# A two-layer encoder trunk on one core: two gate/up groups of three FFN stages taken together by Strassen's scheme, and weights split 1024 columns at a time

## The chip, the core and the metric

The kernel is one program on one core of a Trainium2 chip. The metric is the device time of one execution in microseconds (us), lower is better. Three runs of the kernel before are shown below, beside one profiled execution.

## What is computed

The input x has 256 tokens of 1024 values. Each of the two layers does: a half-step SwiGLU block, a mixer (self attention and attention to a memory, with one input and one output projection), and a second half-step SwiGLU block.

```
def swiglu(h, w_gate, w_up, w_down):
    return (jax.nn.silu(h @ w_gate) * (h @ w_up)) @ w_down
...
    h = rmsnorm(x, ffn1_norm[i])
    x = x + 0.5 * swiglu(h, ffn1_w_gate[i], ffn1_w_up[i], ffn1_w_down[i])
...
    h = rmsnorm(x, ffn2_norm[i])
    x = x + 0.5 * swiglu(h, ffn2_w_gate[i], ffn2_w_up[i], ffn2_w_down[i])
```

The gate and up weights are 1024 x 2816 each, the down weights 2816 x 1024, all in float32. There are four SwiGLU stages, called here (0,1), (0,2), (1,1) and (1,2) by layer and block.

## The kernel before, in words

**Precision.** Every float32 operand of a product is split into a high part (a cast to fp32r, on ScalarE) and a low part (the difference, on VectorE). `dense` (L405 to L425) then issues three matmuls for one tile of 128 x 128 by 128 x 512: high x high (L416), high x low (L419), low x high (L422).

**Weights.** A chunk is 128 x 2048 float32 (1 MB): four K tiles of 512 columns. `loader` brings chunks into three raw buffers (`NRAW`) with two DMAs of 512 KB each on SP's queue (L281). `split_hi` casts them in four pieces of 512 columns on ScalarE (L321), `split_lo` subtracts in the same four pieces on VectorE (L340). The results go to a ring of four high and four low buffers (`NHL`). So a split can run at most four chunks ahead of TensorE, and a raw buffer comes free when its last low part is written.

**A gate/up stage** has 11 groups of 256 gate and 256 up columns (put side by side, 512 wide), two chunks each (K tiles 0 to 3 and 4 to 7). For each chunk TensorE does two token blocks x four K tiles x three matmuls, 24 in all, into two PSUM banks per group. `evac` then does SiLU (ScalarE, L526), the product (VectorE, L529) and a block transpose (VectorE, L537), writes the result to DRAM (`hd`, L543) and reads it back turned (`hr`, L548), both on SP's queue between the loads of weights. The result is split again (L557, L559).

**The down stage** reads 11 more chunks. Three of them in each of the last three stages (`SEVEN`) are already taken by Strassen's scheme: seven products in place of eight, with weight sums on VectorE (L334).

**What sets the order.** The kernel's author wrote a planner into the program: `Flow` keeps a clock with assumed durations, threads (`loader`, `split_hi`, `split_lo`, `evac`, the mixer's units) are resumed by it, and the order in which they issue is the fixed order of every engine's and queue's instructions. On the chip each of these is taken strictly in that order, and an instruction whose operand isn't there holds up all behind it on its engine. `calm_a` and `calm_v` let a split in only when the planner sees at most 0.4 us of work queued on its engine.

**The side of x.** `prep_half` (L453 to L470) transposes x by TensorE, multiplies by the gain into `y` (L460), casts to `xh` (L463) and subtracts to `xl` (L465).

## Time and profile before

| | |
|---|---|
| Three runs | 964.70, 964.88 (median), 967.41 us |
| Profiled execution | 964.95 us, of which the span of the profile is 963.2 us |
| TensorE busy | 954.8 us (99%), clock granted 1.00 |
| VectorE busy | 745.0 us (77%) |
| ScalarE busy | 567.9 us (59%) |
| DMA | 204.04 MB, 212 GB/s over the span |

In time order the stages lie at about: (0,1) 12 to 195 us, first mixer 195 to 317, (0,2) 317 to 498, (1,1) 498 to 680, second mixer 680 to 781, (1,2) 781 to 963. PE is TensorE, DVE VectorE, ACT ScalarE, POOL GpSimd; SP's queue issues all loads. Matmuls overlap in the pipe, so the mean duration of one is longer than the distance from one to the next; the cost of a matmul in a stream is that distance.

### The profile page before, as it was taken

Reading aid. Unit: us, or ns where it says so; the run is one execution under the profiler, and the core shown is the slowest. Engines: PE = TensorE matmul, PEld = TensorE weight load, DVE = VectorE, ACT = ScalarE, POOL = GpSimd, SP = SyncE. Lnnn points to the kernel's source line nnn. Section 1 sums busy time; section 2 is a strip of 40 time slices with the busy share of each in tenths; the row PEclk is TensorE's granted clock in tenths of the full one; section 3 lists DMA queues with packets and bytes.
Section 4 is the critical chain, followed back from the end, with each engine's and each line's share of the span. In section 5 each row is a group of like instructions: output and inputs, shape, how many; then the busy total and the mean of one; then the engine's idle time right before and its main releaser. Section 6 shows DMA issues by size and latency. Waiting matters only on the chain.

```text
span 963.2 us, 13464 instructions
## 1 busy us (share of the span) xinstructions
PE 954.8 (99%) x4525; PEld 783.9 (81%) x4525; DVE 745.0 (77%) x1569; ACT 567.9 (59%) x1215; POOL 60.5 (6%) x65
## 2 busy tenths in 40 slices
PE   8999999999999999999999999999999999999998
PEld 7888888888777888888888888888787788888886
DVE  6777777788777877759986775797989886776785
ACT  6655555666676655545645555565677765554551
POOL 0000000021210000000000000000343100000000
PEclk9999999999999999999999999999999999999999
DMA  8988877486525479766568777666641468777661
GB/s 282 328 267 285 250 263 246 145 272 208 176 88 175 154 224 284 235 229 205 184 208 254 247 245 220 212 202 219 207 143 44 134 196 283 232 254 225 215 190 44
DMA packets 169295, 204.04 MB, mean 212 GB/s; under 512 B 9673, under 2 KB 144394, under 8 KB 169226
## 3 DMA queue, kind: packets, MB, share of 16 engines
q1 hardware_dynamic: 169226, 203.18, 66.0%
q8 instruction: 35, 0.57, 0.2%
q14 instruction: 34, 0.28, 0.1%
HBM read 188.99 MB, written 14.16 MB: 211 GB/s over the span
## 4 chain that ended last, share of the span: by engine, by line
PE 94%; DVE 3%; ACT 1%; DMA 1%; SPq 0%; issue 0%; ACTq 0%
PE gu L422 17%; PE gu L416 17%; PE gu L419 17%; PE acc L416 9%; PE acc L422 9%; PE acc L419 9%; PE pj L422 3%; PE pj L416 3%; PE pj L419 3%; PE xtp L429 1%; PE ptp L429 1%; PE S L1139 1%; PE AV L1220 1%; PE m L422 1%; PE m L419 1%; PE m L416 1%
## 5 line engine op out<-in xcount | busy, mean ns | idle before, releaser
L340 DVE TENSOR_TENSOR lo<-raw,hi 128x512 fp32r<-128x512 f32 x647 | 413.7, 684 | 103.9 <-ACT hi L321 100.0
L321 ACT CAST hi<-raw 128x512 fp32r<-128x512 f32 x647 | 361.7, 618 | 219.0 <-PE gu L422 123.6
L422 PE MATMUL gu<-hi,xl 128*128 128x512 f32 x704 | 274.3, 390 | 0.0
L416 PE MATMUL gu<-hi,xh 128*128 128x512 f32 x704 | 274.1, 389 | 0.0
L419 PE MATMUL gu<-lo,xh 128*128 128x512 f32 x704 | 274.0, 389 | 0.0
L422 PEld LDWEIGHTS gu<-hi,xl 128*128 128x128 f32 x704 | 132.2, 188 | 27.4
L419 PEld LDWEIGHTS gu<-lo,xh 128*128 128x128 f32 x704 | 132.2, 188 | 27.3
L416 PEld LDWEIGHTS gu<-hi,xh 128*128 128x128 f32 x704 | 132.2, 188 | 27.3
L416 PE MATMUL acc<-hi,ht 128*128 128x512 f32 x280 | 109.6, 391 | 0.0
L422 PE MATMUL acc<-hi,ht 128*128 128x512 f32 x280 | 109.2, 390 | 0.0
L419 PE MATMUL acc<-lo,ht 128*128 128x512 f32 x280 | 109.1, 390 | 0.0
L422 PE MATMUL pj<-hi,xl 128*128 128x512 f32 x160 | 64.5, 403 | 0.0
L419 PE MATMUL pj<-lo,xh 128*128 128x512 f32 x160 | 63.6, 397 | 0.0
L416 PE MATMUL pj<-hi,xh 128*128 128x512 f32 x160 | 63.5, 397 | 0.0
L422 PEld LDWEIGHTS acc<-hi,ht 128*128 128x128 f32 x280 | 52.6, 188 | 11.0
L419 PEld LDWEIGHTS acc<-lo,ht 128*128 128x128 f32 x280 | 52.6, 188 | 10.7
L416 PEld LDWEIGHTS acc<-hi,ht 128*128 128x128 f32 x280 | 52.6, 188 | 10.7
L526 ACT ACTIVATE sil<-gu,xr 128x256 f32<-128x256 f32 x88 | 41.5, 472 | 28.6 <-PE gu L422 28.6
L559 DVE TENSOR_TENSOR ht<-hr,ht 128x512 fp32r<-128x512 f32 x35 | 24.1, 687 | 32.2 <-ACT ht L557 32.2
L529 DVE SCALAR_TENSOR_TENSOR h<-gu,xr,sil 128x256 f32<-128x256 f32 x88 | 42.2, 479 | 5.8 <-ACT sil L526 4.5
L557 ACT CAST ht<-hr 128x512 fp32r<-128x512 f32 x35 | 21.6, 618 | 41.9 <-DMA hr<-hd 41.8
L436 POOL TENSOR_TENSOR xr<-v,nhalf 128x1 f32<-128x1 f32 x12 | 8.4, 698 | 502.3 <-DVE v L434 502.3
(191 smaller groups left out, 1069.0 us busy)
## 6 DMA issues: line engine op xcount, KB each, us to landing
raw<-in_ffn_w_down_dram SPq DMA_DIRECT2D x176, 256.0 KB, 4.1
raw<-in_ffn_w_gate_dram SPq DMA_DIRECT2D x86, 512.0 KB, 4.3
raw<-in_ffn_w_up_dram SPq DMA_DIRECT2D x86, 512.0 KB, 5.5
raw<-in_w_in_dram SPq DMA_DIRECT2D x32, 512.0 KB, 4.1
hd<-hb SPq DMA_DIRECT2D x44, 256.0 KB, 2.3
hr<-hd SPq DMA_DIRECT2D x44, 256.0 KB, 5.3
raw<-in_w_out_dram SPq DMA_DIRECT2D x8, 1024.0 KB, 5.0
raw<-in_w_mem_kv_dram SPq DMA_DIRECT2D x4, 1024.0 KB, 5.4
```

The costliest lines, as they stand in the source:

```text
L321: nc.scalar.copy(out=c.part(0, q), in_=c.block(q))
L340: nc.vector.tensor_sub(c.part(1, q), c.block(q), c.part(0, q).bitcast(F32))
L416: nc.tensor.matmul(out=ps, lhsT=xh, rhs=wh, start=start, stop=False)
L419: nc.tensor.matmul(out=ps, lhsT=xh, rhs=wl, start=False, stop=False)
L422: nc.tensor.matmul(out=ps, lhsT=xl, rhs=wh, start=False, stop=stop)
L429: nc.tensor.transpose(out=dst, in_=src, identity=flip if flipped else ident)
L526: nc.scalar.activation(sil, ps[tb][:, 0:256], AF.Silu, scale=xt.r[tb])
L529: nc.vector.scalar_tensor_tensor(out=h, in0=ps[tb][:, 256:512], scalar=xt.r[tb], in1=sil, op0=ALU.mult, op1=ALU.mult)
L557: nc.scalar.copy(out=hi, in_=src)
L559: nc.vector.tensor_sub(lo, src, hi.bitcast(F32))
L1139: nc.tensor.matmul(out=ss[e][:, pr, :nk], lhsT=q[rows, pr, :], rhs=k[rows, pr, :], start=i == 0, stop=i == len(passes) - 1)
L1220: nc.tensor.matmul(out=av[64 * e:64 * e + 64, pr, :], lhsT=vsrc(kb, pr, e), rhs=pts[e][:, pr, kb, :], start=(kb == 0), stop=(kb == nb - 1))
```

## The change

Two things are changed.

**Strassen in the gate/up stage.** In stages (0,2), (1,1) and (1,2), groups 3 and 4 are computed together (`PAIR`). Their weights are four chunks: 11 (group 3, K tiles 0 to 3), 21 (group 3, K tiles 4 to 7), 12 (group 4, K tiles 0 to 3) and 22 (group 4, K tiles 4 to 7). With the two token blocks on the other side this is a 2 x 2 by 2 x 2 product, done in seven products of four K tiles x three matmuls (12 each) in place of eight. Three of the right sides are plain chunks, four are sums T1 = 12 - 11, T3 = 22 - 12, T2 = 22 - T1 and T4 = 21 - T2 (`wsum`), made on VectorE in float32 four pieces at a time and split like a chunk. Each of these seven fills one of the four buffers of the high/low ring. Four forms of x are made at the start of the stage (`pair_forms`: four sums of `y`, four casts, four differences). The seven products `m1` to `m7` each go to a PSUM bank of their own, and `pair_sums` adds them up (one copy on ScalarE, seven additions on VectorE) before the usual evacuation. Groups 0 to 2 go ahead of the pair as before; chunks of groups 5 to 8 stand between its products (called p in the order: 11, m1, p, 12, m5, p, 22, m7, p, m6, p, m3, p, p, 21, m2, p, m4). Raw chunks 11, 12 and 22 stay in their raw buffers until a later product has read them too.

**Width of a split.** All chunks but the first two, and but the sums, are cast and subtracted 1024 columns at a time in place of 512.

```diff
@@ the weight blocks and the two splitting threads
+    class Item:
+        def __init__(self, raws, uses=8):
+            self.raws, self.uses = raws, uses
+            self.hi = self.lo = None
+            self.hit, self.lot, self.st = [None] * 7, [None] * 7, [None] * 4
+            self.n, self.frees, self.takes, self.gives = 1, 1, 0, 0
+            self.sums, self.t = [], []
+            self.index = len(items)
+            w = 1 if len(items) < 2 else 2
+            self.units = [(self.own(q, w), q, w, None) for q in range(0, 4, w)]
+            items.append(self)
+        def own(self, q, w=1, i=0):
+            return lambda: self.raws[i].raw[:, q * 512:(q + w) * 512]
+        def part(self, lo, q, w=1):
+            t = (self.lo if lo else self.hi)[q // 4]
+            return t[:, q % 4 * 512:(q % 4 + w) * 512]
+    chunks, items = [], []
...
-            for q in range(7 if c.seven else 4):
+        for i, it in enumerate(items):
+            yield lambda: hl_left[0] >= it.n and all(r.raw is not None for r in it.raws)
+            hl_left[0] -= it.n
+            yield max(r.early or r.arrive for r in it.raws)
+            it.hi, it.lo = ([whl.tile([P, 2048], F32R, tag=x, name=f"{x}{i}_{j}") for j in range(it.n)]
+                            for x in ("hi", "lo"))
+            for src, q, w, dep in it.units:
                 if q == 2:
-                    yield c.arrive
-                if c.seven and q >= 3:
-                    yield lambda: c.tt[q - 3] is not None
-                    yield c.tt[q - 3]
+                    yield max(r.arrive for r in it.raws)
+                if dep is not None:
+                    yield lambda: it.st[dep] is not None
+                    yield it.st[dep]
                 yield calm_a(i)
-                nc.scalar.copy(out=c.part(0, q), in_=c.block(q))
-                c.hit[q] = flow.act(512)
+                nc.scalar.copy(out=it.part(0, q, w), in_=src())
+                t = flow.act(512 * w)
+                it.hit[q:q + w] = [t] * w
...
+            if it.sums:
+                yield lambda: all(r.raw is not None for r in it.raws) and g2.left >= it.takes + 2
+                yield max(r.arrive for r in it.raws)
+                it.t += [g2.take([P, 512], F32, "wsum") for _ in range(it.takes)]
+                for j, (x, y) in enumerate(it.sums):
                     yield calm_v(i)
-                    nc.vector.tensor_sub(t[j], x, y)
-                    c.tt[j] = flow.dve(512)
-            for q in range(7 if c.seven else 4):
-                yield lambda: c.hit[q] is not None
-                yield c.hit[q]
+                    nc.vector.tensor_sub(it.t[j], x(), y())
+                    it.st[j] = flow.dve(512)
+            for src, q, w, dep in it.units:
+                yield lambda: it.hit[q] is not None
+                yield it.hit[q]
                 yield calm_v(i)
-                nc.vector.tensor_sub(c.part(1, q), c.block(q), c.part(0, q).bitcast(F32))
-                c.lot[q] = flow.dve(512)
-                if q == 3:
-                    raw_left[0] += 1
-            if c.seven:
-                g2.give(4)
+                nc.vector.tensor_sub(it.part(1, q, w), src(), it.part(0, q, w).bitcast(F32))
+                t = flow.dve(512 * w)
+                it.lot[q:q + w] = [t] * w
+            raw_left[0] += it.frees
+            g2.give(it.gives)
@@ which groups, and the products
+    PAIR = {(0, 1): None, (0, 2): 3, (1, 1): 3, (1, 2): 3}
...
+    def pair_items(raws):
+        r11, r12, r22, r21 = raws
+        def sums(need, x, y, held=None):
+            it = Item(need, 4)
+            it.t, it.takes = (held.t, 0) if held else ([], 4)
+            at_ = lambda v, j: it.own(j, 1, v) if isinstance(v, int) else (lambda: v.t[j])
+            it.sums = [(at_(x, j), at_(y, j)) for j in range(4)]
+            it.units = [((lambda j=j: it.t[j]), j, 1, j) for j in range(4)]
+            return it
...
+        def m1():
+            made["b11"] = plain(r11, 0)
+        def m5():
+            made["t1"] = sums([r12, r11], 0, 1)
+        def m7():
+            made["t3"] = sums([r22, r12], 0, 1)
+            made["t3"].gives = 4
+        def m6():
+            made["t2"] = sums([r22], 0, made["t1"], made["t1"])
+            made["t2"].frees = 0
+        def m3():
+            made["b22"] = plain(r22, 1)
+        def m2():
+            made["b21"] = plain(r21, 0)
+        def m4():
+            made["t4"] = sums([r21], 0, made["t2"], made["t2"])
+            made["t4"].gives = 4
+        return made, dict(m1=m1, m5=m5, m7=m7, m6=m6, m3=m3, m2=m2, m4=m4)
@@ the order of the blocks in a gate/up stage
+            rest = [w for w in work if w[0] not in (pair, pair + 1)]
+            n = 2 * pair
+            p = iter(rest[n:])
+            work = rest[:n]
+            for x in ("11", "m1", "p", "12", "m5", "p", "22", "m7", "p", "m6", "p", "m3", "p", "p", "21", "m2", "p", "m4"):
+                work.append(next(p) if x == "p" else x)
+            work += list(p)
+            blocks = {"11": (pair, 0), "12": (pair + 1, 0), "22": (pair + 1, 1), "21": (pair, 1)}
+            raws = [Chunk(parts(*blocks[x])) for x in ("11", "12", "22", "21")]
@@ the sides of x, the sums of the products and one product
+            yield lambda: len(xt.y) == 4 and g4.left >= 4
+            y = xt.y
+            fm = [g4.take([P, 2, 4, P], F32R, "xf") for _ in range(4)]
+            for j, op, o, a, b in ((0, nc.vector.tensor_add, (1, 1), (1, 0), (1, 1)),
+                                   (2, nc.vector.tensor_sub, (1, 0), (0, 0), (1, 0)),
+                                   (1, nc.vector.tensor_sub, (0, 0), (1, 1), (0, 0)),
+                                   (3, nc.vector.tensor_sub, (0, 1), (0, 1), (0, 0))):
+                yield lambda: flow.free["V"] <= flow.now + SLACK
+                op(y[o], y[a], y[b])
+                flow.dve(512)
+            for j, o in ((0, (1, 1)), (2, (1, 0)), (1, (0, 0)), (3, (0, 1))):
+                yield lambda: flow.free["A"] <= flow.now + SLACK
+                nc.scalar.copy(out=fm[j][:, 0], in_=y[o])
+                yield flow.act(512)
+                yield lambda: flow.free["V"] <= flow.now + SLACK
+                nc.vector.tensor_sub(fm[j][:, 1], y[o], fm[j].bitcast(F32)[:, 0])
+                xt.ft[j] = flow.dve(512)
+                g2.give()
+            xt.fm = fm
...
+            yield lambda: "m6" in mt and "m7" in mt
+            yield mt["m6"]
+            yield g2.has(3)
+            u2, w, v = (g2.take([P, 512], F32, "gu_v") for _ in range(3))
+            plus(u2, u, pb["m6"])
+            banks.give()
+            plus(w, u2, pb["m5"])
+            banks.give()
+            t = plus(v, w, pb["m7"])
+            pps[1][1], pend[1][1] = v, t
+            plus(u2, u2, pb["m7"])
+            banks.give()
+            for m, (g, tb), x in (("m3", (1, 0), w), ("m2", (0, 0), u), ("m4", (0, 1), u2)):
+                yield lambda: m in mt
+                yield mt[m]
+                t = plus(x, x, pb[m])
+                banks.give()
+                pps[g][tb], pend[g][tb] = x, t
...
+            name, left = {"m1": ("b11", (0, 0)), "m5": ("t1", 0), "m7": ("t3", 2), "m6": ("t2", 1), "m3": ("b22", 3),
+                          "m2": ("b21", (0, 1)), "m4": ("t4", (1, 1))}[m]
...
+                if isinstance(left, int):
+                    flow.until(lambda: xt.ft[left] is not None)
+                    f = xt.fm[left]
+                    fh, fl, ready = f[:, 0, k, :], f[:, 1, k, :], lambda: xt.ft[left]
+                else:
+                    tb, kk = left[0], 4 * left[1] + k
+                    fh, fl, ready = xt.h[tb][:, kk, :], xt.l[tb][:, kk, :], lambda: xt.t[tb][kk]
+                t = dense(pb[m], fh, fl, ready, pit[name], k, k == 0, k == 3)
```

The first place is VectorE in the gate/up stage of (0,2), from the split of chunk 58 on (`lo58`; 57 is 11 of the pair, 59 is 12). Before:

```order
L340 TENSOR_TENSOR lo58_0_3565<-raw58_3464,hi58_0_3564 128x512
L340 TENSOR_TENSOR lo58_0_3565<-raw58_3464,hi58_0_3564 128x512
L529 SCALAR_TENSOR_TENSOR h_3588<-gu1_3471,xr_3003,sil_3572 128x256
L559 TENSOR_TENSOR ht_3576<-hr_3533,ht_3576 128x512
L537 STREAM_TRANSPOSE hb_3554<-h_3588 128x2x4x32
L340 TENSOR_TENSOR lo58_0_3565<-raw58_3464,hi58_0_3564 128x512 x2
L923 TENSOR_TENSOR ropew_1273<-ropew_1273 128x64
L905 TENSOR_SCALAR ropew_1273<-ropew_1273 128x64
L340 TENSOR_TENSOR lo59_0_3617<-raw59_3500,hi59_0_3616 128x512
L907 TENSOR_TENSOR ropew_1273<-ropew_1273 128x64
```

Now:

```order
L344 TENSOR_TENSOR lo58_0_3347<-raw58_3278,hi58_0_3346 128x1024
L613 SCALAR_TENSOR_TENSOR h_3365<-gu1_3259,xr_2813,sil_3353 128x256
L643 TENSOR_TENSOR ht_3359<-hr_3322,ht_3359 128x512
L621 STREAM_TRANSPOSE hb_3336<-h_3365 128x2x4x32
L344 TENSOR_TENSOR lo58_0_3347<-raw58_3278,hi58_0_3346 128x1024
L338 TENSOR_TENSOR wsum_3382<-raw59_3311,raw57_3204 128x512
L338 TENSOR_TENSOR wsum_3383<-raw59_3311,raw57_3204 128x512
L338 TENSOR_TENSOR wsum_3384<-raw59_3311,raw57_3204 128x512
L338 TENSOR_TENSOR wsum_3385<-raw59_3311,raw57_3204 128x512
L344 TENSOR_TENSOR lo59_0_3399<-wsum_3382,hi59_0_3398 128x512
L344 TENSOR_TENSOR lo59_0_3399<-wsum_3383,hi59_0_3398 128x512
L344 TENSOR_TENSOR lo59_0_3399<-wsum_3384,hi59_0_3398 128x512
```

The split of chunk 59 is now four sums, which read two raw buffers, and four narrow subtractions (three are shown); the split of 58 has two wide subtractions in place of four. `ht` is the turned SwiGLU result, `h` and `hb` belong to the evacuation of group 1.

The second place is SP's queue at the same point of the program (`raw60`, issued just ahead, is the plain chunk between m5 and m7; 61 is 22 of the pair, 62 to 64 are plain). Before:

```order
L543 DMA hd_3603<-hb_3554 128x512
L281 DMA raw61_3606<-in_ffn2_w_gate_dram 128x4x256
L281 DMA raw61_3606<-in_ffn2_w_up_dram 128x4x256
L548 DMA hr_3634<-hd_3603 128x4x128
L281 DMA raw62_3642<-in_ffn2_w_gate_dram 128x4x256
L281 DMA raw62_3642<-in_ffn2_w_up_dram 128x4x256
L543 DMA hd_3712<-hb_3654 128x512
L281 DMA raw63_3721<-in_ffn2_w_gate_dram 128x4x256
L281 DMA raw63_3721<-in_ffn2_w_up_dram 128x4x256
L548 DMA hr_3742<-hd_3712 128x4x128
L281 DMA raw64_3749<-in_ffn2_w_gate_dram 128x4x256
L281 DMA raw64_3749<-in_ffn2_w_up_dram 128x4x256
```

Now:

```order
L627 DMA hd_3389<-hb_3336 128x512
L632 DMA hr_3413<-hd_3389 128x4x128
L288 DMA raw61_3431<-in_ffn2_w_gate_dram 128x4x256
L288 DMA raw61_3431<-in_ffn2_w_up_dram 128x4x256
L627 DMA hd_3495<-hb_3437 128x512
L288 DMA raw62_3501<-in_ffn2_w_gate_dram 128x4x256
L288 DMA raw62_3501<-in_ffn2_w_up_dram 128x4x256
L632 DMA hr_3521<-hd_3495 128x4x128
L288 DMA raw63_3552<-in_ffn2_w_gate_dram 128x4x256
L288 DMA raw63_3552<-in_ffn2_w_up_dram 128x4x256
L288 DMA raw64_3569<-in_ffn2_w_gate_dram 128x4x256
L288 DMA raw64_3569<-in_ffn2_w_up_dram 128x4x256
```

The number of loads is the same; the read-back `hr` of group 1 now stands ahead of chunk 61, and chunks 63 and 64 are issued one behind the other.

The third place is VectorE in the second mixer, around the softmax difference `pe` of an attention unit (`lo126` splits the last chunk of the input projection, `raw126`; `lo133` the first one of the output projection, `raw127`: in the changed kernel the number at `lo` counts split blocks, the sums among them, and the number at `raw` counts chunks). Before:

```order
L1127 SCALAR_TENSOR_TENSOR oT0_6988<-otp_7132,gcs_104,oT0_6988 128x2x128
L340 TENSOR_TENSOR lo126_0_7031<-raw126_6898,hi126_0_7030 128x512
L713 SCALAR_TENSOR_TENSOR qkn_7172<-pj0_7033,xr_6103,hf_7129 128x512
L1258 RECIPROCAL rs_7180<-sums_7126 128x4
L1261 SCALAR_TENSOR_TENSOR cf_7182<-sums_7126,nlam_109,rs_7180 128x2
L1266 SCALAR_TENSOR_TENSOR pe_7139<-pe_7144,cf_7182,pe_7139 128x128 x2
L804 TENSOR_TENSOR k1_7098<-qktp_7158,k1_7098 128x2x128
```

Now:

```order
L1222 TENSOR_TENSOR m1_6813<-qkn_6789,ropeC_107 128x512
L1226 TENSOR_TENSOR m1_6813<-m1_6813,m2_6812 128x512
L1439 RECIPROCAL rs_6837<-sums_6788 128x4
L1442 SCALAR_TENSOR_TENSOR cf_6839<-sums_6788,nlam_109,rs_6837 128x2
L1447 SCALAR_TENSOR_TENSOR pe_6799<-pe_6803,cf_6839,pe_6799 128x128 x2
L344 TENSOR_TENSOR lo133_0_6829<-raw127_6630,hi133_0_6828 128x1024
L894 SCALAR_TENSOR_TENSOR qkn_6855<-pj0_6713,xr_5841,hf_6808 128x512
L985 TENSOR_TENSOR k1_6767<-qktp_6847,k1_6767 128x2x128
L985 TENSOR_TENSOR q1_6857<-qktp_6847,q1_6857 128x256
```

The weight split among the steps of the attention is now 1024 wide, and it stands behind `pe` in place of ahead of it.

More of the change, by code (lines that the diff above doesn't have):

```diff
@@ L654, in ffn @@
+        if pair is not None:
+            flow.spawn(pair_forms())
+        work = list(plan[l, nm, "work"])
+        if (l, nm) != (0, 1):
+            for tb in range(2):
+                for c in range(2):
+                    plain_chunk(0, c, (tb,))
+            work = work[2:]
+        for w in work:
+            if isinstance(w, str):
+                product(w)
+            else:
+                plain_chunk(*w, range(2))
         flow.until(banks.has(4))
         acc = Acc()
-        nxt = None if gc_next is None else Xt()
+        nxt = None if gc_next is None else Xt(nm == 2 and PAIR[l + 1, 1] is not None)
```

164 lines of the change are left out of this document (95 added, 69 removed).

## Prediction

> **What bounds the kernel now.** First the page: the span, the busy shares, the chain of waits that ended last, and the costliest groups.
>
> ```profile
> span 963.2 us, 13464 instructions
> ...
> PE 954.8 (99%) x4525; PEld 783.9 (81%) x4525; DVE 745.0 (77%) x1569; ACT 567.9 (59%) x1215; POOL 60.5 (6%) x65
> ...
> PE 94%; DVE 3%; ACT 1%; DMA 1%; SPq 0%; issue 0%; ACTq 0%
> ...
> L340 DVE TENSOR_TENSOR lo<-raw,hi 128x512 fp32r<-128x512 f32 x647 | 413.7, 684 | 103.9 <-ACT hi L321 100.0
> L321 ACT CAST hi<-raw 128x512 fp32r<-128x512 f32 x647 | 361.7, 618 | 219.0 <-PE gu L422 123.6
> L422 PE MATMUL gu<-hi,xl 128*128 128x512 f32 x704 | 274.3, 390 | 0.0
> ```
>
> TensorE is the bound: 94% of the chain. The splits (L340, L321) wait for others, ScalarE's mostly for TensorE to free a ring buffer. A matmul's 390 ns cannot be its price, since 4525 of them would take longer than the span; so I read the distance between starts, in the timeline of TensorE inside stage (0,2). The first and the last of 37 rows that follow one another without a gap:
>
> ```profile
> 369.67 0.39 PE L416 MATMUL gu<-hi,xh 128*128 128x512 f32 x1
> ...
> 377.83 0.39 PE L416 MATMUL gu<-hi,xh 128*128 128x512 f32 x1
> ```
>
> 8.16 us over 36 distances is 0.2267 us for a matmul of 512 columns. Then all that TensorE waited for anybody, in the whole run:
>
> ```profile
> PE warm L1425 <- POOL ident masks.py:199: 1.4, 1, 1.4
> PE xtp L429 <- DMA x<-in_x_dram: 1.1, 2, 0.9
> PE ptp L429 <- DVE pe L1266: 0.7, 2, 0.6
> PE acc L416 <- DVE oT L1127: 0.4, 1, 0.4
> PE qktp L429 <- DVE m L1045: 0.4, 1, 0.4
> PE qktp L429 <- ACT PT L1153: 0.4, 1, 0.4
> ```
>
> It is 4.4 us, and none of it is in a SwiGLU stage. So a matmul that goes there shortens the run by its distance, as long as the splits keep ahead. The windows show how much room they have (columns: window, length, then busy time of PE, PEld, DVE, ACT, POOL, granted clock, DMA share, GB/s): the two halves of (0,2), and the second mixer.
>
> ```profile
> 320.00:450.00 130.00, 130.00 (x577) 107.65 (x576) 98.16 (x219) 71.28 (x142) 0.94 (x1) 1.00 0.74 233
> 450.00:501.00 51.00, 51.00 (x235) 42.22 (x234) 44.20 (x77) 30.71 (x61) 0.55 (x1) 1.00 0.60 191
> ...
> 681.00:770.00 89.00, 87.02 (x502) 68.89 (x501) 80.96 (x184) 63.48 (x180) 31.09 (x27) 1.00 0.41 133
> ```
>
> **Part 1: matmuls removed.** A pair of groups takes four chunks x 24 = 96 matmuls now, and seven products x 12 = 84 then. 12 fewer in each of three stages is 36 x 0.2267 = 8.16 us off the path. From the profiled execution: 964.95 - 8.16 = 956.79 us. (It stands 0.07 us from the median 964.88, which I neglect.)
>
> **Part 2: work added on VectorE.** Per stage: 4 sums and 4 differences for the forms of x, 16 weight sums, 16 narrow differences of the four T blocks, 7 additions of products: 47 operations 512 wide; and 6 wide differences for the three plain right sides. It removes 16 narrow differences. Prices, from the timelines of VectorE and ScalarE and the groups by form:
>
> ```profile
> 335.20 2.50 DVE L340 TENSOR_TENSOR lo<-raw,hi 128x512 fp32r<-128x512 f32 x4 [1.54 <-ACT hi L321]
> ```
>
> ```profile
> 334.55 2.18 ACT L321 CAST hi<-raw 128x512 fp32r<-128x512 f32 x4 [2.94 <-PE gu L422]
> ```
>
> ```profile
> L586 DVE TENSOR_TENSOR h<-sf,h 128x512 fp32r<-128x512 f32 x9 | 6.2, 686 | 0.3
> L573 DVE TENSOR_TENSOR sf<-hr 128x128 f32<-128x128 f32 x18 | 5.2, 287 | 13.4 <-DMA hr<-hd 13.4
> L586 DVE TENSOR_TENSOR h<-hr,h 128x256 fp32r<-128x256 f32 x9 | 3.6, 395 | 0.0
> ```
>
> In a row, one difference costs (2.50 - 0.684) / 3 = 0.605 us, one cast (2.18 - 0.618) / 3 = 0.52. No row is 1024 wide. The step from 128 to 512 columns is 1.04 ns a column, from 256 to 512 1.14: 512 more columns cost 0.53 to 0.58, so a wide difference takes 1.14 to 1.19 in a row against 1.21 for two narrow ones. I take 1.14, since the first step is read over the longer reach, and 1.05 at most for a wide cast (two narrow ones in a row). Added: 47 x 0.605 + 6 x 1.14 - 16 x 0.605 = 25.6 us per stage. Saved by width: 18 other gate/up chunks, 8 plain down chunks and a half of 3 more, (2 x 26 + 3) x 0.07 = 3.9. Net 21.7 us, and VectorE idles 181 - 98.16 - 44.20 = 38.6 in this stage. On the sum it fits; what decides is the lead inside the stretch of the pair.
>
> **Part 3: does the lead last?** Now it is long. The block that VectorE finished at 337.7 (row above: 335.20 + 2.50) is the one whose first matmul starts here, 13 us later:
>
> ```profile
> 350.63 0.39 PE L416 MATMUL gu<-hi,xh 128*128 128x512 f32 x1
> ```
>
> In the stretch from m1 to m4 TensorE takes 7 x 12 + 7 x 24 = 252 matmuls, 57.1 us. A T block gives it only 2.72 us of work but costs VectorE 8 x 0.605 = 4.8, and a raw buffer is held by chunks 11, 12 and 22, so that the plain chunks p1 to p4 (groups 5 and 6) go mostly through one buffer, each load waiting for the split of the one before. I sum VectorE's queue in its new order with these rows (DMA issues and landings in part of (0,2), and the landing of all loads of 320 to 450; the last number of a row is us from issue to landing):
>
> ```profile
> raw<-in_ffn_w_gate_dram SPq DMA_DIRECT2D x11, 512.0 KB, 4.8
> raw<-in_ffn_w_up_dram SPq DMA_DIRECT2D x11, 512.0 KB, 5.3
> hd<-hb SPq DMA_DIRECT2D x6, 256.0 KB, 2.2
> hr<-hd SPq DMA_DIRECT2D x6, 256.0 KB, 5.4
> ```
>
> ```profile
> DMA to landing us min/median/max: 3.0/4.8/6.4
> ```
>
> ```profile
> L529 DVE SCALAR_TENSOR_TENSOR h<-gu,xr,sil 128x256 f32<-128x256 f32 x88 | 42.2, 479 | 5.8 <-ACT sil L526 4.5
> L537 DVE STREAM_TRANSPOSE hb<-h 128x256 f32<-128x256 f32 x88 | 38.7, 440 | 1.0
> ```
>
> Zero is the start of m1; an evacuation step counts 0.40 and a transpose 0.36 (each less the 0.08 that overlaps). p1 was split at -6.1: its ring buffer came free at -10.8, when group 1 ended, and ht and an evacuation stand in between. Then T1's sums and differences, 4.8, to -1.3. Here VectorE waits: the four `sf` sums of group 1 need hr, which SP issues behind p2's load and hd (-5.2, + 2.2, + 0.45 to issue, + 5.4 = 2.9). p2 has its first half at 5.3. After group 1's forms p2 is done at 7.9; T3 4.8, to 12.8. p3's load could start only at 7.9, with p2's buffer: 7.9 + 0.5 + 5.3 = 13.7, cast 1.05, first half at 15.9, second 17.1. ht 0.6, T2's sums and differences with two evacuations, 4.8 + 1.5, to 24.1, its first quarter at 21.5. p4 follows at once: 25.2 and 26.4. Against TensorE:
>
> ```
> block               T1     p2     T3     p3     T2     p4     m3's 22
> first part ready   -3.1    5.3   10.9   15.9   21.5   25.2    27.5
> first needed        8.2   10.9   16.3   19.0   24.5   27.2    32.6
> lead               11.3    5.6    5.4    3.1    3.0    2.0     5.1
> ```
>
> So the lead shrinks from 11 to 2 us and then grows again, since 22 is already there and four plain chunks follow. I forecast that it lasts, with little to spare: 0.3 us of waits a stretch, 1.0 in all, because two landings at 6.4 in place of 5.3 would use up the 2.0 and I hold that for the exception. The bank copies and additions in `pair_sums` stand behind p4 and p5, where the lead is over 4.
>
> **Part 4: wide splits elsewhere.** In the SwiGLU stages the first half of a block comes about one narrow piece later (0.5 us each on cast and difference), against a lead of 13: nothing. In the second mixer VectorE is busy 80.96 of 89 us, and TensorE waits there for about 1.9 us (the last four rows of its waits). Its splits, in the groups of 684 to 752:
>
> ```profile
> L340 DVE TENSOR_TENSOR lo<-raw,hi 128x512 fp32r<-128x512 f32 x31 | 20.8, 701 | 0.8 <-ACT hi L321 0.8
> ```
>
> Merged they save some 15 x 0.07 = 1.1 us of a nearly full queue; against this a step of the attention that comes just after a split has begun waits up to 0.53 longer. By the rows the gain is at most the 1.9 that TensorE waits. For the loss I take five such delays on the path at half of 0.53, and ten whole ones as the far end: 1.3 and 5.3. I take 0, between, as the queue is nearer to full than to idle.
>
> The Trainium skill (Perfetto Trace Analysis, section Optimizing Scalar/DVE Operations) says that larger operations help where the engine is saturated, and that where it isn't, but makes others wait, breaking operations up lets work be done sooner. By that page the merge speaks against the change where VectorE is 77% busy (whole run) and for it where it is 91% busy (this window); no run here shows yet which of them rules. Its VectorE: DVE Perf Modes (section on the TRN2 errata) prices a float32 operation on two tensors at (N + 151) / 0.96: an estimate of 1.22 us for 1024 columns alone; for 512 it gives 0.691, and the trace agrees with 0.684 to 0.688.
>
> **Sum.** 964.95 - 8.16 + 1.0 + 0 = 957.8 us.
>
> **Rivals.**
> 1. The lead runs out in part. For it: 2.0 us at p4, and a longest landing of 1.1 above the one that I used, on two loads and one hr in the chain. Against it: the median landing of the gate half is 4.8. Slips of 3 to 4 us leave 1 to 2 us of wait a stretch, 3 to 6 in all: 959.8 to 962.8. Chance 0.17.
> 2. Slower than before: the one free raw buffer becomes the bound. Each plain chunk then costs load, cast and two differences in series, 0.5 + 5.3 + 1.05 + 2.28 = 9.1 us, where TensorE allows it 8.16 (a product and a chunk). It decides when the chain from p1 to p4 slips by more than 2.0 + 3.7 us, which needs landings near 8 us; the rows end at 6.4. With 4 us lost a stretch: 964.95 - 8.16 + 12 = 968.8. Chance 0.06.
> 3. Merged splits hold up the second mixer (the rule above): with the delays of part 4 between its two ends, 2.7: 957.8 + 2.7 = 960.5. Chance 0.08.
> 4. The mixer gains instead, the whole 1.9, and no stretch waits: 956.8 - 1.9 = 954.9. Chance 0.03.
> 5. The removed matmuls were not on the path: the chain and the waits leave no room for it. Below 0.01.
>
> **How the numbers follow.** The forecast keeps 0.66. 0.3% is 2.9 us, about what a measurement of this kernel can tell; the line lies at 962.0. Forecast, rivals 3 and 4 and two thirds of rival 1 are below it: 0.88. A third of rival 1 and little else is within 0.3%: 0.06. Slower is rival 2: 0.06. The range runs from 955.5 (no waits and most of the mixer's gain) to 962.5 (rival 1 nearly whole), and leaves out rival 2 and the ends of 1 and 4.
>
> **What would show it.** 36 fewer matmuls at an unchanged 0.227 us; a table of TensorE's waits with no row for the pair's banks, or rows under 1 us; wide differences at about 1.2 us and the wait for hr ahead of `sf`. In the second mixer TensorE's waits stay under 4 us. I am wrong if the stretch from m1 to m4 takes over 59 us in any stage, or if the other stages change by more than a us.

## The result and the profile after

The changed kernel takes 981.21 us (median of four runs, 979.62 to 983.73) beside 964.79 us before: a ratio of 1.0165 (1.0151 to 1.018). The forecast was 957.8 with a range up to 962.5; it is wrong by the sign. First the page of the changed kernel: span, busy shares, chain of waits, costliest groups.

```profile
span 977.8 us, 12960 instructions
...
PE 956.4 (98%) x4489; PEld 777.8 (80%) x4489; DVE 794.5 (81%) x1389; ACT 562.5 (58%) x957; POOL 64.5 (7%) x65
...
PE 52%; DVE 22%; DMA 17%; issue 3%; ACT 3%; SPq 2%; DVEq 0%; ACTq 0%
...
L344 DVE TENSOR_TENSOR lo<-raw,hi 128x1024 fp32r<-128x1024 f32 (+1 forms) x326 | 380.5, 1191 | 29.7 <-ACT hi L326 29.0
L326 ACT CAST hi<-raw 128x1024 fp32r<-128x1024 f32 (+1 forms) x326 | 322.6, 1026 | 135.5 <-DMA raw<-in_ffn_w_up_dram 50.3
```

The 36 matmuls are gone (4525 to 4489), and still the span grew by 14.6 us. TensorE holds 52% of the chain in place of 94%; VectorE (22%) and DMA (17%) have most of the rest. By TensorE's timeline the three gate/up stages with a pair became 2.1 to 2.8 us shorter (12 matmuls are 2.7 us), and the down stages behind them 11.7, 5.7 and 4.8 us longer. What TensorE waits for, and then the wait for the read-back on ScalarE and the DMA issues of it, after:

```profile
PE acc L499 <- DVE lo L344: 7.6, 7, 1.5
PE m L496 <- DVE h L613: 4.5, 3, 2.2
...
PE m L499 <- DVE lo L344: 0.7, 1, 0.7
...
PE gu L499 <- DVE lo L344: 0.3, 1, 0.3
```

```profile
ACT ht L641 <- DMA hr<-hd: 111.7, 24, 9.2
```

```profile
hd<-hb SPq DMA_DIRECT2D x44, 256.0 KB, 4.7
hr<-hd SPq DMA_DIRECT2D x44, 256.0 KB, 3.9
```

The waits are in the down stage (`acc` and `m` are its banks), and no row names the banks of the pair. The 4.5 us for `h` are no wait for a split: L613 is the product in the evacuation of the last gate/up group, and as I read the program a bank for the Strassen block comes free behind it. Before, the row of ScalarE was:

```profile
ACT ht L557 <- DMA hr<-hd: 41.8, 25, 2.8
```

`ht` is the split of the SwiGLU result that was written to DRAM (`hd`) and read back (`hr`). ScalarE now stands 111.7 us before it, up to 9.2 at once. Here is that longest wait, in (0,2) where the gate/up stage ends: ScalarE's timeline, then SP's queue, then four rows of VectorE's (start, length, engine, operation; in brackets the idle time before).

```profile
421.45 3.18 ACT L326 CAST hi<-raw 128x1024 fp32r<-128x1024 f32 x3
424.53 0.47 ACT L610 ACTIVATE sil<-gu,xr 128x256 f32<-128x256 f32 x1
434.20 0.62 ACT L641 CAST ht<-hr 128x512 fp32r<-128x512 f32 x1 [9.20 <-DMA hr<-hd]
434.73 0.47 ACT L610 ACTIVATE sil<-gu,xr 128x256 f32<-128x256 f32 x1
439.12 0.62 ACT L641 CAST ht<-hr 128x512 fp32r<-128x512 f32 x1 [3.92 <-DMA hr<-hd]
439.64 1.56 ACT L326 CAST hi<-raw 128x512 fp32r<-128x512 f32 x2
```

```profile
416.39 9.12 SPq L288 DMA_DIRECT2D raw<-in_ffn_w_down_dram  x8
425.56 0.58 SPq L627 DMA_DIRECT2D hd<-hb  x1
426.24 2.54 SPq L288 DMA_DIRECT2D raw<-in_ffn_w_down_dram  x4
430.56 0.37 SPq L632 DMA_DIRECT2D hr<-hd  x1
```

```profile
421.05 0.76 DVE L621 STREAM_TRANSPOSE hb<-h 128x256 f32<-128x256 f32 x2
...
434.86 0.69 DVE L643 TENSOR_TENSOR ht<-hr,ht 128x512 fp32r<-128x512 f32 x1 [3.24 <-ACT ht L641]
...
441.00 0.69 DVE L344 TENSOR_TENSOR lo<-raw,hi 128x512 fp32r<-128x512 f32 x1
...
441.71 1.22 DVE L344 TENSOR_TENSOR lo<-raw,hi 128x1024 fp32r<-128x1024 f32 x1
```

`hb` is ready at 421.8, but `hd` stands on SP's queue behind eight loads and is issued at 425.56; `hr` waits there until `hd` has landed (430.56), and lands at 434.20. ScalarE has nothing to do but the `ht` in front of it, and the casts of the next chunk stand behind two of them, until 439.64. That chunk is the first Strassen block of the down stage. Its first low part ends at 441.69. TensorE has begun the block at 440.64 and waits 0.71 us for that part:

```profile
440.64 0.39 PE L496 MATMUL m<-hi,h 128*128 128x512 f32 x1
441.74 0.50 PE L499 MATMUL m<-lo,h 128*128 128x512 f32 x1 [0.71 <-DVE lo L344]
```

The lead of the splits over TensorE in (0,2), worked out from the timelines of VectorE and TensorE: from the end of a block's first low part to the first matmul that takes it. This is the second one of the block, 0.23 us behind its start; the prediction counted to the start. A lead of 0.1 means that TensorE had to wait. The columns are T1 to the pair's 22, then the last four chunks of gate/up, then blocks of the down stage, the Strassen chunks being the 2nd, 5th and 7th there. The run e13, below, is the changed kernel in its own order, with the splits of what was read back taking a constant.

```
                 T1    p2   T3   p3   T2   p4   22  | last four of gate/up    | down: 1st, 1st Strassen, ..., 7th, last
prediction      11.3   5.6  5.4  3.1  3.0  2.0  5.1 |
before                                              | 15.0  15.0  15.0  15.0  |  14.2   8.3        6.5   1.6
after           10.1   4.0  3.9  1.6  1.5  0.6  3.8 |  1.3   3.9   3.4   5.5  |   8.3   0.1        0.1   0.1
e13             11.3   7.8  6.4  4.8  4.7  3.8  6.9 |  5.1   7.4   6.3   8.5  |  11.2   7.7        6.2   2.3
```

In the kernel before, the lead is 15 us in these last four chunks, and the down stage itself spends it down to 1.6.

The waits that the table of waits names are not the whole loss. For each matmul of the SwiGLU stages that follows another of the same stage I took the distance between their starts less 0.2267 us: 15.2 us lie at 12 rows that show a wait, and 8.3 us at 55 rows that show none (e13: nothing and 1.4). Of these 8.3 us, 3.8 lie in two series behind waits, of which this is the first, and most of the rest in single rows right behind a wait or at waits too short to be shown:

```profile
486.70 0.50 PE L499 MATMUL acc<-lo,ht 128*128 128x512 f32 x1 [1.17 <-DVE lo L344]
...
489.16 0.80 PE L499 MATMUL acc<-lo,ht 128*128 128x512 f32 x1 [1.50 <-DVE lo L344]
...
490.61 0.63 PE L499 MATMUL acc<-lo,ht 128*128 128x512 f32 x1
491.04 0.63 PE L502 MATMUL acc<-hi,ht 128*128 128x512 f32 x1
491.46 0.63 PE L496 MATMUL acc<-hi,ht 128*128 128x512 f32 x1
```

```profile
489.60:494.90 5.30, 5.30 (x16) 4.13 (x16) 3.19 (x5) 0.54 (x1) 0.00 (x0) 0.50 0.87 252
495.00:498.00 3.00, 3.00 (x15) 2.44 (x14) 2.22 (x6) 1.25 (x3) 0.00 (x0) 1.00 0.81 284
```

The distance is 0.43 us in place of 0.227, and the granted clock (third number from the end) is 0.50 for these 5.3 us, then 1.00 again. So the waits cost their own length and then, all told, about half as much again: 15.2 + (8.3 - 1.4) = 22.1 us, against 977.8 - 955.0 = 22.8 between the spans of this kernel and e13.

### The profile page after: what moved, and what is told of

It reads as the page before. It is cut to its first block, busy times and chain, and to the rows that moved or that the text cites. A ratio compares the mean times of both kernels' runs of the same rounds, so it can differ in the third digit from the quotient of the medians.

```text
span 977.8 us, 12960 instructions
## 1 busy us (share of the span) xinstructions
PE 956.4 (98%) x4489; PEld 777.8 (80%) x4489; DVE 794.5 (81%) x1389; ACT 562.5 (58%) x957; POOL 64.5 (7%) x65
## 4 chain that ended last, share of the span: by engine, by line
PE 52%; DVE 22%; DMA 17%; issue 3%; ACT 3%; SPq 2%; DVEq 0%; ACTq 0%
DVE lo L344 12%; PE gu L502 7%; PE gu L499 7%; PE gu L496 7%; DMA hd<-hb 5%; PE acc L499 5%; PE acc L502 5%; PE acc L496 5%; DMA raw<-in_ffn_w_up_dram 4%; DMA hr<-hd 4%; DMA raw<-in_ffn_w_down_dram 3%; PE pj L496 3%; PE pj L502 3%; PE pj L499 3%; SPq L288 2%
## 5 line engine op out<-in xcount | busy, mean ns | idle before, releaser
L344 DVE TENSOR_TENSOR lo<-raw,hi 128x1024 fp32r<-128x1024 f32 (+1 forms) x326 | 380.5, 1191 | 29.7 <-ACT hi L326 29.0
L326 ACT CAST hi<-raw 128x1024 fp32r<-128x1024 f32 (+1 forms) x326 | 322.6, 1026 | 135.5 <-DMA raw<-in_ffn_w_up_dram 50.3
L499 PE MATMUL gu<-lo,xh 128*128 128x512 f32 x608 | 237.0, 390 | 0.4 <-DVE lo L344 0.3
L502 PE MATMUL gu<-hi,xl 128*128 128x512 f32 x608 | 237.0, 390 | 0.0
L496 PE MATMUL gu<-hi,xh 128*128 128x512 f32 x608 | 236.8, 389 | 0.0
L499 PEld LDWEIGHTS gu<-lo,xh 128*128 128x128 f32 x608 | 114.1, 188 | 25.0 <-DVE lo L344 1.3
L496 PEld LDWEIGHTS gu<-hi,xh 128*128 128x128 f32 x608 | 114.2, 188 | 23.6
L502 PEld LDWEIGHTS gu<-hi,xl 128*128 128x128 f32 x608 | 114.2, 188 | 23.4
L641 ACT CAST ht<-hr 128x512 fp32r<-128x512 f32 x35 | 21.7, 620 | 111.9 <-DMA hr<-hd 111.7
L326 ACT CAST hi<-wsum 128x512 fp32r<-128x512 f32 x84 | 49.1, 619 | 37.5 <-DVE wsum L338 37.2
L496 PEld LDWEIGHTS acc<-hi,ht 128*128 128x128 f32 x280 | 53.4, 191 | 11.7 <-ACT hi L326 0.5
L344 DVE TENSOR_TENSOR lo<-wsum,hi 128x512 fp32r<-128x512 f32 x84 | 53.2, 681 | 0.0
L516 POOL TENSOR_TENSOR xr<-v,nhalf 128x1 f32<-128x1 f32 x12 | 11.6, 972 | 496.8 <-DVE v L514 322.2
```

The source lines that it names most:

```text
L326: nc.scalar.copy(out=it.part(0, q, w), in_=src())
L344: nc.vector.tensor_sub(it.part(1, q, w), src(), it.part(0, q, w).bitcast(F32))
L496: nc.tensor.matmul(out=ps, lhsT=xh, rhs=wh, start=start, stop=False)
L499: nc.tensor.matmul(out=ps, lhsT=xh, rhs=wl, start=False, stop=False)
L502: nc.tensor.matmul(out=ps, lhsT=xl, rhs=wh, start=False, stop=stop)
L516: nc.gpsimd.tensor_tensor(out=dst, in0=v[:, :n], in1=nhalf[:, :n], op=ALU.pow)
```

## The experiments

Four theories, as the expectations name them. **A**: the pair's work on VectorE spends the lead, and that is the loss. **B**: wide splits make those wait who need a first part. **C**: the read-back; the fixed order sets `ht` on ScalarE at the time at which the planner thinks that `hr` has landed (3.0 us for `hd`, 4.0 for `hr`); on the chip it comes later, and the casts of weights stand behind it. **D** came up on the way: whatever changed in the order when the planner's numbers were changed, and not the wait. Each ratio is to the kernel before on the same chip.

**One part alone, and the other.** e1 has the wide splits without the pair; e2 the pair with all splits 512 wide.

```diff
-    PAIR = {(0, 1): None, (0, 2): 3, (1, 1): 3, (1, 2): 3}
+    PAIR = {(0, 1): None, (0, 2): None, (1, 1): None, (1, 2): None}
```

> The change with no pair in any stage: only the splits 1024 columns wide (and the planner's new lists) are left. Theory A (spent lead: the pair makes VectorE fall behind, its lead is not back when the down stage begins, and TensorE waits there): no slower than the kernel before, 962.5 to 965.5 us, and the table of TensorE's waits has no row over 1 us for the down blocks. Rival B (width: wide splits bring the first half of each block later and hold up the steps behind them, and that makes the waits of the down stage): 970 us or more, with the waits of TensorE for lo in the down stages.

```diff
-            w = 1 if len(items) < 2 else 2
+            w = 1
```

> The change with the pair in all three stages, but every split 512 columns wide as before. Theory A (spent lead): VectorE has 3.9 us more to do per stage than in the changed kernel, so as slow or slower: 981 to 993 us. Rival B (width): 957 to 963 us. Rival C (the order that the planner wrote at the end of the gate/up stage, with read-backs hr behind loads that wait for raw buffers, whatever the lead): about the changed kernel, 978 to 984.

e1: 966.91 us, 1.0015 (1.0003 to 1.0028). e2: 974.41 us, 1.009 (1.007 to 1.0111). ScalarE's wait for the read-back in the one and in the other:

```profile
ACT ht L641 <- DMA hr<-hd: 138.0, 32, 7.4
```

```profile
ACT ht L641 <- DMA hr<-hd: 62.1, 22, 6.6
```

Neither part alone gives the loss, nor do the two add up to it (1.5 + 9.0 against 16.4 us). e1 lies 1.4 us above the range of A but shows none of the waits that B asks for; the time of e2 lies in the range of none of the three. Width alone makes the wait for the read-back longer than in the changed kernel, and it costs next to nothing, since the lead stays at 9 to 14 us in the gate/up stages; TensorE waits for no split in e1. The pair with 62.1 us of that wait, against 111.7 in the changed kernel, costs 9 us. So by these two runs it is the spent lead and the long wait together that cost.

**The place of the pair, and the other user of the lead.** e3 takes groups 1 and 2 as the pair, e4 takes one of three Strassen chunks out of the down stages, e7 all of them (27 matmuls more, 6.1 us).

```diff
-    PAIR = {(0, 1): None, (0, 2): 3, (1, 1): 3, (1, 2): 3}
+    PAIR = {(0, 1): None, (0, 2): 1, (1, 1): 1, (1, 2): 1}
```

> The change with the pair two groups earlier (groups 1 and 2 in place of 3 and 4), so that four more plain chunks (21.8 us of TensorE) stand between the pair and the down stage. Theory A (spent lead): VectorE needs about 3.7 us for a plain chunk against 5.44 of TensorE, so some 7 us more of lead are back when the down stage begins, and the waits there shrink to a few us: 958 to 968 us. Rival C (order at the end of the gate/up stage, whatever the lead): 976 to 983. Rival B (width): 978 to 983.

```diff
-    SEVEN = {(0, 1): (), (0, 2): (1, 4, 6), (1, 1): (1, 4, 6), (1, 2): (1, 4, 7)}
+    SEVEN = {(0, 1): (), (0, 2): (4, 6), (1, 1): (4, 6), (1, 2): (4, 7)}
```

> The change with one Strassen block fewer in each of the last three down stages (the first one, chunk 1, is taken plainly). VectorE is spared 4 weight sums, 4 narrow differences and the forms of that block, about 6 us per stage, TensorE has 3 matmuls more, 0.7 us per stage. Theory A (spent lead): the waits of the down stage shrink by about 4 to 6 us per stage: 966 to 972 us. Rivals B and C: 980 to 984 us.

```diff
-    SEVEN = {(0, 1): (), (0, 2): (1, 4, 6), (1, 1): (1, 4, 6), (1, 2): (1, 4, 7)}
+    SEVEN = {(0, 1): (), (0, 2): (), (1, 1): (), (1, 2): ()}
```

> The change with no Strassen block in any down stage (pairs in the gate/up stages only). TensorE has 27 matmuls more, 6.1 us in all; VectorE has about 19 us less in each of three down stages. Theory A (spent lead): the down stage no longer needs the lead, TensorE waits only around the pairs, 1 to 3 us in all: 963 to 967 us. Theory C (read-back): the waits at the start of the down stage stay, since the read-backs stand there as before: 975 to 985 us.

e3: 994.61 us, 1.0297 (1.0272 to 1.0321). e4: 978.84, 1.0136 (1.0111 to 1.016). e7: 968.6, 1.0039 (1.0025 to 1.0054). TensorE's waits for splits in e3 and in e4:

```profile
PE pair_m L499 <- DVE lo L344: 7.0, 5, 1.9
PE gu L499 <- DVE lo L344: 6.2, 7, 2.4
PE acc L499 <- DVE lo L344: 5.8, 4, 2.0
```

```profile
PE gu L499 <- DVE lo L344: 8.6, 6, 3.6
PE pair_m L499 <- DVE lo L344: 2.9, 1, 2.9
```

e3 lies outside every range that I gave, and e4 too: with one chunk less the order changed, and the waits moved from the down stage into the gate/up stage. In e7 ScalarE's wait is longer still (145.7 us), but no Strassen chunk of the down stage draws on the lead, and TensorE waits 1.1 us for splits. C alone had expected 975 to 985 there and fails; that fits a read-back which costs only where the lead is spent. The fit is loose: e7 has 9 matmuls fewer than the kernel before (2.0 us) and takes 3.2 us more, 1.6 above A's range, and its trace is of the fastest of five executions (964.58 us), so most of that is not explained.

**The read-back.** e5 tells the planner later times for it; e6 puts `hd` and `hr` on GpSimd's queue, away from the loads.

```diff
             nc.sync.dma_start(out=hd.rearrange("a i b x -> (a i) (b x)"), in_=hb.rearrange("p b t f j -> p (b t f j)"))
-            yield flow.now + 3.0
+            yield flow.now + 5.5
...
             nc.sync.dma_start(out=hr, in_=hd.rearrange("a i b x -> (i b) a x"))
-            yield flow.now + 4.0
+            yield flow.now + 5.0
```

> The change with two numbers of the planner altered: it counts 5.5 us (in place of 3.0) for hd and 5.0 us (in place of 4.0) for hr in the evacuation of a group, so that the casts of the read-back (ht) stand later in ScalarE's order; no instruction is added or taken away. Theory C (read-back: the way from hb over hd to hr takes longer than the order allows, ScalarE stands at ht with the casts of weights behind it, and what lead the pair has left is lost there): ScalarE's wait for hr falls from 112 to under 60 us, and the time to 962 to 970 us. Theory A (spent lead: VectorE's added work alone): 977 to 985 us.

```diff
-            nc.sync.dma_start(out=hd.rearrange("a i b x -> (a i) (b x)"), in_=hb.rearrange("p b t f j -> p (b t f j)"))
+            nc.gpsimd.dma_start(out=hd.rearrange("a i b x -> (a i) (b x)"), in_=hb.rearrange("p b t f j -> p (b t f j)"))
...
-            nc.sync.dma_start(out=hr, in_=hd.rearrange("a i b x -> (i b) a x"))
+            nc.gpsimd.dma_start(out=hr, in_=hd.rearrange("a i b x -> (i b) a x"))
```

> The change with hd and hr issued by GpSimd's queue in place of SP's, in the same planned order otherwise; no work is added or taken away. Theory C (read-back): they no longer stand behind loads that wait for a raw buffer, so hd and hr land sooner, ScalarE's wait for hr falls to under 80 us, and the time to 960 to 973 us, if this queue is as quick to issue. Theory A (spent lead): 977 to 985 us.

e5: 957.32 us, 0.9922 (0.9907 to 0.9937). e6: 973.64, 1.0086 (1.0071 to 1.0101). In e5, 4.7 us below C's range, ScalarE's wait is about half, and the one wait of TensorE for a split is 0.3 us:

```profile
ACT ht L641 <- DMA hr<-hd: 59.2, 22, 6.9
```

```profile
PE acc L499 <- DVE lo L344: 0.3, 1, 0.3
```

e6 has `hd` land in 3.6 us (median), but the order is the old one and ScalarE still waits 89.7 us, where C had expected under 80, and the time is 0.6 us above C's range: a third of the loss is back, no more.

**Width once more, with the order mended.** e8 is e5 with all splits narrow and `LAT` at 2.5 us in place of 1.5, which is what the planner counts from the end of a load's transfer to its landing (no delay between engines, as the second expectation calls it); e11 is the same with the wide splits.

```diff
-            w = 1 if len(items) < 2 else 2
+            w = 1
...
-    LAT = 1.5
+    LAT = 2.5
...
-            yield flow.now + 3.0
+            yield flow.now + 5.5
...
-            yield flow.now + 4.0
+            yield flow.now + 5.0
```

> The change with splits 512 columns wide, with 5.5 and 5.0 us counted for hd and hr, and 2.5 us (in place of 1.5) for the landing of a load behind its transfer. Theory C (read-back) with the width as its second cause: 957 to 966 us. Theory A (spent lead): no better than the narrow pair of before, 973 to 980 us.

> As e8 (read-back counted 5.5 and 5.0 us, 2.5 us of delay between engines in the planner) but with the wide splits of the change. C: no waits for splits, so width is worth nothing either way: 956 to 958.5. B (wide splits hold up whoever waits for a first part): 959 or more, over 2 us above e8's 956.9.

e8: 956.92 us, 0.9921 (0.9906 to 0.9936). e11: 957.05, 0.9914 (0.9887 to 0.994). B falls: with the order right, width is worth nothing that these runs can tell. These two and e5 beat both kernels.

**The planner's numbers elsewhere.** e9 gives e5's 5.5 and 5.0 us to the kernel before; e12 gives 1.5 and 2.5 us to the changed one.

> The kernel before, with the planner counting 5.5 and 5.0 us for hd and hr in place of 3.0 and 4.0, as in e5. C (the read-back holds up ScalarE, and this costs only where the lead is spent): TensorE waits for no split in the kernel before, so there is nothing to win: 963.5 to 966.5 us, with ScalarE's wait for hr under its 41.8 us. Rival D (the later order is worth some 8 us whatever the kernel, and the Strassen pair gave nothing in e5): 955 to 960.

> The changed kernel with the planner counting 1.5 and 2.5 us for hd and hr in place of 3.0 and 4.0: hr and ht stand earlier still. C: ScalarE's wait for hr rises above 150 us from 111.7, and TensorE's waits with it: 986 to 1000. A: the order of the read-back is beside the point, 978 to 984.

e9: 968.62 us, 1.0029 (1.0017 to 1.0041), and ScalarE's wait and TensorE's there:

```profile
ACT ht L557 <- DMA hr<-hd: 108.6, 32, 6.2
PE acc L419 <- DVE lo L340: 2.6, 3, 1.1
```

D falls: the later order brings the kernel before nothing. But C's step that later numbers shorten the wait falls as well: here they lengthened it from 41.8 us, since the loads, casts and read-backs were all set anew. It cost 0.3%, 2.1 us above C's range, with the lead of the kernel before in hand. e12: 1072.02 us, 1.1089 (1.1058 to 1.1119), far over the 1000 that C allowed; ScalarE's wait is 229.2 us, and TensorE waits for splits in the pair's banks, the gate/up and the down stages, and once 11.6 us for a load of another tensor (`grow`). The direction is C's; I did not settle how its 91 us divide.

**The wait taken out, the order kept.** In e10, e13 and e14 no instruction moves. e10 reads an old `hd`, so that `hr` waits for no write; in e13 the splits of what was read back take a constant; e14 is e13 with the pair at 1, in the order of e3.

```diff
-            nc.sync.dma_start(out=hr, in_=hd.rearrange("a i b x -> (i b) a x"))
+            nc.sync.dma_start(out=hr, in_=old[0].rearrange("a i b x -> (i b) a x"))
```

> The changed kernel in exactly its own order on every engine, but every hr after the first reads what the first group of the program left in DRAM, so that no hr waits for its hd (the result is left wrong by this: the down stages work on the first group's values). C (it is the wait for the read-back itself): ScalarE's wait for hr falls from 111.7 to under 70 us, TensorE's waits for splits go below 5 us in all, 957 to 964. A (the lead is spent by the pair's own work on VectorE) and D (it was something else in the order that e5 changed): 976 to 982.

```diff
-            src = hr.rearrange("p a (c j) -> p c a j", c=4)
+            src = ident.unsqueeze(1).to_broadcast([P, 4, P]).rearrange("p a (c j) -> p c a j", c=4)
```

> The changed kernel in its own order, every read-back still issued, but the operations that split what was read back take a constant in place of hr (the down stages so work on a constant, and the result is left wrong): no engine waits for hd or hr at all. e10 left 98.5 us of ScalarE's wait and 964.8 us. C: with the last of the wait gone the time is that of the kernels whose order is right, 956 to 959 us, and no split is waited for by over 0.5 us. A (the lead that the pair spends has a price of its own, whatever the read-back does): 962 to 966, with waits for splits at the down stage's Strassen blocks.

> As e13 with the pair as groups 1 and 2 (e3 took 994.6 us with the true read-back, and the lead was spent from the stretch of the pair on). C: the place of the pair does not matter by itself, 956 to 960 us. A: the pair early in the stage spends a lead that is shorter there, 963 to 985, with waits in the banks of the pair.

e10: 964.83 us, 0.999 (0.9977 to 1.0004). e13: 956.73, 0.9903 (0.9886 to 0.992). e14: 980.34, 1.0148 (1.0117 to 1.0178). The page of e13:

```profile
span 955.0 us, 12947 instructions
...
PE 947.1 (99%) x4489; PEld 776.4 (81%) x4489; DVE 794.3 (83%) x1389; ACT 564.6 (59%) x957; POOL 64.3 (7%) x65
...
PE 93%; DVE 5%; DMA 1%; ACT 1%; issue 0%; SPq 0%; DVEq 0%; ACTq 0%
```

VectorE does the same work as in the changed kernel (794.3 against 794.5 us busy), in the same order, and 24.5 us are gone: for the change as it stands the wait for the read-back is shown to be needed for the loss, as C has it, and VectorE's added work alone (A) does not give it. e10 came out just above C's range; its `hr` still keeps ScalarE for 98.5 us where C had expected under 70 (it lands in 5.5 us by itself), and 2.4 us of TensorE's waits for splits of the down stage remain. What e14 waits for:

```profile
PE gu L499 <- DVE lo L344: 14.2, 11, 2.8
```

So with the pair as groups 1 and 2, where the lead at T1 is 1.6 us, no read-back is needed to spend the rest. The time is in A's range, but the waits are not in the banks of the pair, and in that stretch of (0,2) (328 to 404 us) ScalarE waits 13.2 us for raw loads: that it is VectorE's work alone is not shown. Of e3's 994.61 - 956.73 = 37.9 us, 23.6 are there without the read-back and 14.3 come with it.

## Why the prediction was wrong, step by step

**Part 1** was right: 36 x 0.2267 us off the path gives 956.79 us, and e13 took 956.73, e5, e8 and e11 956.9 to 957.3.

**Part 2** was right. Two wide differences in a row took 2.36 us and one alone 1.22 (the row of 441.71), so the second 2.36 - 1.22 = 1.14, as I took it:

```profile
425.96 2.36 DVE L344 TENSOR_TENSOR lo<-raw,hi 128x1024 fp32r<-128x1024 f32 x2
```

The pair added 794.5 - 721.6 (e1) = 72.9 us of VectorE's busy time, 24.3 a stage where I took 25.6.

**Part 3**, the stretch: the sum ran 1.2 to 1.6 us above the measured leads (1.4 to 1.8, counted to the start of the block as it did), and its shape held, down to 0.6 at p4 and up again at 22. The stretch from m1 to m4 took 57.1 us in each of the three stages, as forecast, and no bank of the pair was waited for. **The step that failed is the end of this part: the lead "shrinks from 11 to 2 us and then grows again, since 22 is already there and four plain chunks follow".** The sum stopped at the block of m3, ahead of m4, and counted `ht` as 0.6 us of VectorE's work and its wait on ScalarE at nothing. Behind m4 the lead stayed at 1.3 to 8.3 and was 0.1 at the first Strassen block of the down stage. Two things were left out. That ScalarE feeds the casts through one fixed queue with `ht` in it, which waits up to 9.2 us for SP's queue, `hd` and `hr` in series. And that the lead had another user, the down stage: in the kernel before it falls from 15 us to 6.5 by the third Strassen chunk, and to 1.6 at the last chunk (the last three chunks are taken side by side, a quarter at a time), so a lead that "lasts" through the pair has still to be there behind it. In e13 it does grow again as the sentence has it, to 5.1 to 8.5 us in the last four chunks of the gate/up stage; that was enough, by 2.3 us for the first part of the last chunk and 0.5 for its second half (before: 1.6 and 0.4).

As long waits on ScalarE cost little where more of the lead was left: 138.0 us in e1, 145.7 in e7 and 108.6 in e9, and these kernels stand 0.15, 0.39 and 0.29% above the kernel before. In the changed kernel 111.7 cost 24.5 us. The row "ACT ht" of before, 41.8 us, was there to be read, and I took it for idle time of an engine off the path.

**Part 4**, "In the SwiGLU stages ... nothing", was nearly right on the time (e1 took 1.5 us more) and missed an effect: the width cost TensorE nothing by a later first half, but merging the splits moved the loads, casts and read-backs against each other, and ScalarE's wait went from 41.8 to 138.0 us in e1. In the second mixer the forecast of 0 held: TensorE's waits there sum to 1.9 us before and 1.4 after, and its length changed by 0.1 us. Of the two rules of the Trainium skill (Perfetto Trace Analysis, section Optimizing Scalar/DVE Operations) neither decides here: e8 and e11 differ by 0.13 us. The estimate of 1.22 us for a difference of 1024 columns from VectorE: DVE Perf Modes agrees with the row of 441.71, 1.22 us.

**The rivals.** Rival 1 was right that the lead runs out, but had it do so inside the stretch and at 3 to 6 us in all. Rival 2 had the sign, at 968.8, but not the cause: in e13 ScalarE waits for landings of the loads of the gate/up stage as much as in the changed kernel (51.4 against 50.3 us for the up half), and TensorE does not feel it. My alarms stood at the wrong place: the stretch, which I had summed, stayed at 57.1 us, and (0,1) and the two mixers changed by 0.3 us at most; neither watched the down stage behind a pair.

## What to carry to other kernels

A lead of one engine over another is one account with several users. Before spending it, list all who draw on it up to the point where it is filled again, and every wait that a feeding engine can have in that time, in-order neighbours among them; a wait that costs nothing today is only as cheap as the lead that hides it. To price such a wait, keep the order and feed the waiting operation from data that is already there, as e13 does; changing the order to avoid it mixes two things.

## What was not expected of the hardware

TensorE's clock fell to half after short waits. In (0,2) of the changed kernel it did so inside the second of two, of 1.17 and 1.50 us (486.70 and 489.16 above), and stayed there up to 494.9:

```profile
488.15:489.10 0.95, 0.00 (x0) 0.00 (x0) 0.95 (x2) 0.95 (x2) 0.00 (x0) 0.50 1.08 382
```

In e14 a single one of 2.26 us was enough:

```profile
367.18 0.50 PE L499 MATMUL gu<-lo,xh 128*128 128x512 f32 x1 [2.26 <-DVE lo L344]
```

```profile
367.20:370.60 3.40, 3.40 (x9) 2.66 (x10) 3.40 (x5) 2.52 (x4) 0.00 (x0) 0.56 0.13 23
371.00:375.00 4.00, 4.00 (x19) 3.31 (x18) 4.00 (x6) 0.02 (x1) 0.00 (x0) 1.00 0.93 316
```

One of 2.18 us in (0,2) of the changed kernel was not: the granted clock stayed at 1.00 behind it.

```profile
448.34 0.50 PE L496 MATMUL m<-hi,h 128*128 128x512 f32 x1 [2.18 <-DVE h L613]
```

```profile
448.40:452.00 3.60, 3.60 (x16) 2.99 (x17) 3.57 (x6) 1.58 (x2) 0.00 (x0) 1.00 0.30 98
```

The Trainium skill (TensorE: Matmul & The Clock Gate, Part 1) has the clock drop after an idle window of about 3.4 us. No wait here was that long, so by these rows the clock can fall without one, and not every wait of some 2 us brings it.

The clock records of all the traces show what seems to decide. In each trace the half-speed stretches begin on a grid of 3.41 us and last whole steps of it while the program runs: in the changed kernel 488.05 to 494.88 us (two steps) and 672.37 to 675.78 (one), with 54 steps between their starts. Taking every step of the 16 traces behind the first 30 us that ran at full clock, TensorE had idled for 1.68 us or more in each of the 29 steps that a fall followed, and for 1.75 us at most in each of the 4317 that none followed. So about half a step of idle time decides, and not the length of a wait: the 2.26 us of e14 lie inside one step (364.2 to 367.6), while the 2.18 us are cut at 447.09 into 0.93 and 1.25. Of the 6.9 us that the changed kernel loses beside its 15.2 us of waits, 3.8 lie in the two half-speed stretches.

A DMA of 256 KB between SBUF and DRAM took 2.3 us from issue to landing in the median of the kernel before and 4.7 us in the changed one, for the same `hd`. Of the one wait of 9.2 us, 0.56 went to its place on SP's queue, 4.95 to `hd` and 3.64 to `hr`.
